# Token mixers: a lane's own next step traced at a higher priority for VectorE, ScalarE and GpSimd

## The chip, the core and the metric

The kernel runs on one core of a Trainium2 chip. The metric is the device time of one execution in microseconds (us). The core's engines are TensorE (PE, matrix products), VectorE (DVE), ScalarE (ACT, functions by table), GpSimd (POOL) and SyncE (SP, which issues the DMAs here). Each takes its own instructions in a fixed order; what must wait for another engine waits on a semaphore, and everything behind it on that engine waits too.

## The reference

A model of two blocks over 512 tokens of width 1024 in float32. The first block mixes tokens in four groups side by side, each 256 wide, and ends with a convolutional gated feed-forward; the second has a short convolution, a gated feed-forward, latent attention and another one. The change lies in the first block's mixers:

```python
def token_mix(h, w_in, ...):
    p = (h @ w_in).astype(jnp.float32)
    (fox_qkv, fox_f, gdn_qkv, gdn_b, gdn_a, gdn_z, hg_q, hg_f, hg_i, hg_g,
     gla_qk, gla_v, gla_gk, gla_g) = jnp.split(p, _cut_points(IN_SIZES), axis=-1)
    ...
    o_a = rms_norm(fox_attention(q, k, split_heads(v, FOX_HEADS), log_f), fox_on_g)
    ...
    o_b = gated_delta_chunked(l2norm(split_heads(q, GDN_HEADS)), l2norm(split_heads(k, GDN_HEADS)),
                              split_heads(v, GDN_HEADS), g, beta)
    ...
    o_c = gla_chunked(jax.nn.silu(split_heads(hg_q, HG_HEADS)), k_in, split_heads(hg_i, HG_HEADS),
                      log_forget, HG_DK ** -0.5)
    ...
    o_d = gla_chunked(split_heads(q, GLA_HEADS), split_heads(k, GLA_HEADS), split_heads(gla_v, GLA_HEADS),
                      split_heads(log_a, GLA_HEADS), GLA_DK ** -0.5)
    ...
    return jnp.concatenate([merge_heads(o_a), merge_heads(o_b), merge_heads(o_c), merge_heads(o_d)], axis=-1)
```

`gated_delta_chunked` solves a triangular system in chunks of 64 tokens, `gla_chunked` needs the products q·k with a decay for each pair of positions.

## The kernel before, in words

Activations lie with features on the partitions, 512 tokens on the free axis. A large product (128 rows of the result) takes eight steps over the 1024 inputs, three matmuls each: the weights `raw` come by DMA, ScalarE rounds them to `wh` (L111) and VectorE takes the rest `wl` (L112), and the matmuls are wh·xh, wh·xl and wl·xh. They gather in a PSUM tile `mm`, which an eviction on VectorE scales into SBUF (L901 for most, L927 a gate, L935 ahead of a convolution, L228).

While the 28 blocks of `w_in` are multiplied, the mixers run beside them in `Mix.conduct` (L751 on). There are three lanes, each a list of generators that follow one another: l (`hg` and `gla`, both through `la`), g (the delta rule, `gdn`) and f (attention, `fox`). The running generator of a lane is a `Strand` in the list `strands`; the ends of the mixers (normalising and gating, `finish`) run as further generators in `self.beside`. Each generator yields the time after which its next step is due by the planner's clock `self.clk`. In every round `conduct` either lets one due generator trace its next step (L804, `t = next(due.gen, None)`) or traces one step of a `w_in` product. Both lie in a `manual_schedule` for TensorE (L1556): TensorE's order is the order of tracing. On VectorE, ScalarE and GpSimd the order is made by the framework's scheduler: among instructions that are ready by its own model it takes the one with the lowest priority number, and that number counts up as the program is traced. So of two that are ready, the one traced earlier goes first.

Each lane has two PSUM tiles in turn (`lps`, `gps`, `fps`; L642 to L644) and temporaries `s`, `u`, `sq` in rings of three or four.

The steps that matter here:

- `la` makes the score products between k and q of a chunk in seven levels. `la_level` (L1287 on) prepares one: GpSimd subtracts the decay (L1299, `s`), ScalarE takes two exponentials of it (L1300, L1301), GpSimd multiplies k by one half (L1303, `lw`), and VectorE multiplies q by the other half, one instruction for each head (L1310, `lbd`, two or four). Then TensorE multiplies `lw` and `lbd` into an `lps` tile, and the result is copied into the scores `lat` under a mask on VectorE (L1361), or on ScalarE at the first level (L1359). The level after the next is prepared behind that copy. Ahead of the levels stand the products lps<-lq,lk with their masking (L1334), the running sums `lg` (L1338), and in `hg` the copy of the values `lv` out of an `lps` tile on ScalarE (L1268).
- `gdn` makes for each of two heads a decay matrix `gmt` (four exponentials on ScalarE, L1088), the weighted products `gat` and `gmt` (L1031), the copy `gmr` (L1107) and the start `gxt` of the inverse (L1110, L1111); GpSimd scales `gko` (L1115) and later masks `gmt` (L1131). Six rounds follow, each with `gy` (L1137), `gx` (L1141) and `gxt` (L1143) out of `gps` tiles. `gvn` (L1117) is the scaled values. At the end `gst` holds the state.
- `la` ends with the states `lst` (L1401).

Of the kernel before, what the change touches and what calls it, by code (L numbers as in the profile page):

```python
# [1 line left out]

# [1 line left out]

# [659 lines left out]
class Mix(Mla):  # L664
# [93 lines left out]
    def conduct(self, jobs, lanes):  # L758
# [7 lines left out]
        strands = [None] * len(lanes)  # L766
# [6 lines left out]
        while True:  # L773
# [6 lines left out]
            due = next((s for s in live if s.at <= self.clk), None)  # L780

            while held and "mean" in self.over:
                ps, name, post = held.pop(0)
                t = post(ps)
# [16 lines left out]
                        due_row = self.clk + DUE  # L801
            if due and not (dense and self.clk - fed > FEED):
                self.lane = due.rings
                t = next(due.gen, None)  # L804
                self.lane = {}
                due.at = self.clk + (t or 0.0)
                if t is None:
                    if due in strands:
                        strands[strands.index(due)] = None
                        self.over.add(due.name)  # L810
                        ready[due.name] = self.clk
                    else:
                        self.beside.remove(due)
                continue
# [873 lines left out]
```

## Time and profile before

| what | before |
|---|---|
| median of three runs | 1862.54 us (1862.07 to 4696.66) |
| the profiled execution | 1862.47 us, span 1860.8 us |
| TensorE busy | 1822.3 us (98% of the span) |
| VectorE busy | 1050.7 us (56%) |
| ScalarE busy | 737.8 us (40%) |
| GpSimd busy | 194.4 us (10%) |
| stage of the mixers beside w_in | about 50 to 376 us |
| in it: TensorE, VectorE, ScalarE, GpSimd busy | 314.67, 242.96, 149.77, 82.97 us |

How to read it: the profiled execution is one of the program's executions, and its span runs from its first to its last instruction. "Busy" is the time in which an engine executes, and the rest is idle time, most of it waiting. TensorE works nearly all the time, so the idle time of another engine costs nothing unless TensorE waits for it. Two matmuls overlap, so starts are a better measure than the listed durations. The granted clock (PEclk) is the share of full speed that the chip gave TensorE. The time 4696.66 is that of one run of the three and lies far off the two others; the profiled execution is near those two.

### The profile page before, as it was taken

To read this page: it belongs to the slowest core of one execution; us is meant where nothing else is said; L and a number is where in the kernel's file an instruction comes from. 1 tells how busy PE (TensorE), PEld (TensorE's weight loads), DVE (VectorE), ACT (ScalarE), POOL (GpSimd) and SP (SyncE) were. 2 spreads that over 40 slices of the span, in tenths; PEclk is the share of its full clock that TensorE was granted. 3 is DMA by queue.
4 is the path that set the end of the run, shared out by engine and by line. 5 is a ranking of instruction groups with operands and counts; after the bars stand their busy time and mean duration, and the time that the engine had idled before them with its cause. 6 is when DMAs were issued, how large, how long until landed. Compare 5 with 4: busy or idle time off the path is not lost.

```text
span 1860.8 us, 22057 instructions
## 1 busy us (share of the span) xinstructions
PE 1822.3 (98%) x8609; PEld 1501.5 (81%) x8609; DVE 1050.7 (56%) x1627; ACT 737.8 (40%) x1138; POOL 194.4 (10%) x225
## 2 busy tenths in 40 slices
PE   8999999999999999999999999999999999999997
PEld 6787887778888888888888888888777888888886
DVE  7875985767777633455564444333876454444323
ACT  6543544544444422322343233322577333232322
POOL 1510502210000001011200000011011200000001
PEclk9999999999999999999999999999999999999999
DMA  4111101332323333323232323333222222323332
GB/s 167 57 35 46 46 35 35 106 101 91 102 93 100 90 100 94 102 91 102 92 106 92 102 91 102 94 94 97 71 60 74 79 96 97 102 91 99 94 94 76
DMA packets 53223, 162.61 MB, mean 87 GB/s; under 512 B 6528, under 2 KB 13184, under 8 KB 53120
## 3 DMA queue, kind: packets, MB, share of 16 engines
q1 hardware_dynamic: 52992, 161.21, 27.2%
q8 instruction: 67, 1.10, 0.3%
q14 instruction: 36, 0.29, 0.0%
q10 hardware_dynamic: 128, 0.01, 0.0%
HBM read 157.78 MB, written 2.10 MB: 86 GB/s over the span
## 4 chain that ended last, share of the span: by engine, by line
PE 85%; DVE 9%; ACT 3%; issue 1%; POOL 1%; DMA 0%; SPq 0%; DVEq 0%; ACTq 0%; POOLq 0%
PE mm L125 24%; PE mm L127 24%; PE mm L126 24%; PE mm L705 6%; PE gps L705 3%; PE lps L705 1%; PE fps L705 1%; DVE lbd L1310 1%; ACT wh L111 1%; DVE wl L112 1%; DVE lat L1361 1%; PE ps L577 1%; DVE ptl L112 0%; PE ps L165 0%; DVE nm L580 0%
## 5 line engine op out<-in xcount | busy, mean ns | idle before, releaser
L111 ACT ACTIVATE wh<-raw 128x1024 fp32r<-128x1024 f32 (+3 forms) x308 | 308.6, 1003 | 762.6 <-PE mm L126 463.5
L125 PE MATMUL mm<-xh,wh 128*128 128x512 f32 x1336 | 521.8, 391 | 0.4 <-ACT xh L173 0.4
L126 PE MATMUL mm<-xl,wh 128*128 128x512 f32 x1336 | 520.7, 390 | 0.5 <-DVE xl L174 0.5
L127 PE MATMUL mm<-xh,wl 128*128 128x512 f32 x1336 | 519.9, 389 | 0.0
L112 DVE TENSOR_TENSOR wl<-raw,wh 128x1024 fp32r<-128x1024 f32 (+3 forms) x300 | 361.0, 1203 | 224.8 <-ACT wh L111 221.6
L126 PEld LDWEIGHTS mm<-xl,wh 128*128 128x128 f32 x1336 | 250.8, 188 | 54.9 <-DVE xl L174 1.4
L125 PEld LDWEIGHTS mm<-xh,wh 128*128 128x128 f32 x1336 | 250.8, 188 | 53.7 <-issue 1.0
L127 PEld LDWEIGHTS mm<-xh,wl 128*128 128x128 f32 x1336 | 250.8, 188 | 51.9 <-issue 0.2
L125 PE MATMUL mm<-hidh,wh 128*128 128x512 f32 (+1 forms) x614 | 236.7, 386 | 0.0
L127 PE MATMUL mm<-hidh,wl 128*128 128x512 f32 (+1 forms) x614 | 235.3, 384 | 0.0
L126 PE MATMUL mm<-hidl,wh 128*128 128x512 f32 (+1 forms) x614 | 233.8, 381 | 0.0
L127 PEld LDWEIGHTS mm<-hidh,wl 128*128 128x128 f32 x614 | 115.4, 188 | 24.2
L126 PEld LDWEIGHTS mm<-hidl,wh 128*128 128x128 f32 x614 | 115.4, 188 | 23.6
L705 PE MATMUL mm<-xh,wh 128*128 128x512 f32 x291 | 127.7, 439 | 6.6 <-ACT xh L173 5.8
L125 PEld LDWEIGHTS mm<-hidh,wh 128*128 128x128 f32 x614 | 115.5, 188 | 21.9 <-ACT wh L111 0.2
L705 PE MATMUL mm<-xh,wl 128*128 128x512 f32 x291 | 116.0, 398 | 1.6 <-DVE wl L112 1.6
L705 PE MATMUL mm<-xl,wh 128*128 128x512 f32 x291 | 116.1, 399 | 0.4 <-DVE xl L112 0.4
L278 DVE TENSOR_TENSOR u<-mm,rb 128x512 f32<-128x512 f32 x44 | 30.4, 691 | 141.2 <-PE mm L127 141.2
L158 POOL TENSOR_TENSOR z<-z,sq 128x512 f32<-128x512 f32 x31 | 50.9, 1643 | 556.6 <-ACT sq L156 518.9
L274 DVE TENSOR_TENSOR u<-mm,rb 128x512 f32<-128x512 f32 x44 | 30.4, 691 | 90.9 <-PE mm L127 90.8
L111 ACT ACTIVATE hidh<-s 128x512 fp32r<-128x512 f32 x66 | 41.8, 633 | 88.6 <-DVE s L255 57.5
L705 PEld LDWEIGHTS mm<-xh,wh 128*128 128x128 f32 x291 | 56.1, 193 | 18.8 <-ACT xh L173 6.3
(434 smaller groups left out, 2089.2 us busy)
## 6 DMA issues: line engine op xcount, KB each, us to landing
raw<-in_w_a_dram SPq DMA_DIRECT2D x52, 512.0 KB, 3.3
raw<-in_w_b_dram SPq DMA_DIRECT2D x52, 512.0 KB, 3.4
raw<-in_w_up_dram SPq DMA_DIRECT2D x44, 512.0 KB, 3.3
raw<-in_w_in_dram SPq DMA_DIRECT2D x28, 512.0 KB, 3.3
raw<-in_conv_w_in_dram SPq DMA_DIRECT2D x24, 512.0 KB, 3.3
raw<-in_w_down_dram SPq DMA_DIRECT2D x16, 448.0 KB, 3.4
raw<-in_w_a_dram SPq DMA_DIRECT2D x16, 448.0 KB, 3.3
raw<-in_w_b_dram SPq DMA_DIRECT2D x16, 448.0 KB, 3.3
```

The lines of the kernel that those rows point to most:

```text
L111: nc.scalar.activation(out=h, in_=src, func=ACTF.Copy)
L112: (eng or nc.vector).tensor_tensor(out=l, in0=src, in1=h.bitcast(F32), op=ALU.subtract)
L125: nc.tensor.matmul(out=ps, lhsT=h, rhs=xh, start=(k == 0), stop=False)
L126: nc.tensor.matmul(out=ps, lhsT=h, rhs=xl, start=False, stop=False)
L127: nc.tensor.matmul(out=ps, lhsT=l, rhs=xh, start=False, stop=(k == kt - 1))
L158: eng.tensor_tensor(out=acc, in0=acc, in1=sq, op=ALU.add)
L274: nc.vector.tensor_tensor(out=g, in0=ps, in1=r, op=ALU.mult)
L278: nc.vector.tensor_tensor(out=g, in0=ps, in1=r, op=ALU.mult)
L577: nc.tensor.matmul(out=ps[:, :n], lhsT=l[:, qs], rhs=r[:, :n], start=(i == 0), stop=False)
L705: self.nc.tensor.matmul(out=out, lhsT=lhsT, rhs=rhs, start=start, stop=stop)
L1310: nc.vector.tensor_tensor(out=bd[rows, :, h].rearrange("p c (n j) -> p c n j", j=b), in0=c4(q)[rows], in1=c4(d)[rows], op=ALU.mult)
L1361: nc.vector.copy_predicated(out=at.rearrange("p c (n j) -> p c n j", j=2 * b)[:, :, :, b:], mask=self.lmask[:, lv - 1].rearrange("p (n j) ...
```

## The change

One statement of `conduct` is changed. While it lets a lane's running generator trace its next step, the scheduler's priority is set back to that of the program's start (`high_priority()` without an offset), and restored behind the step. The numbers count up from there within the step, so that every lane step begins with the same number, whatever its age. The generators of `beside`, the products of w_in with their splits and evictions, and all that follows keep their numbers. TensorE's order, made by hand, is the same, and so is SyncE's. Line numbers behind the change are two higher.

```diff
--- before.py
+++ after.py
@@ -1,4 +1,4 @@
-from contextlib import ExitStack, contextmanager
+from contextlib import ExitStack, contextmanager, nullcontext
 
 import numpy as np
 
@@ -801,7 +801,9 @@
                         due_row = self.clk + DUE
             if due and not (dense and self.clk - fed > FEED):
                 self.lane = due.rings
-                t = next(due.gen, None)
+
+                with self.tc.high_priority() if due in strands else nullcontext():
+                    t = next(due.gen, None)
                 self.lane = {}
                 due.at = self.clk + (t or 0.0)
                 if t is None:
```

What it does to the order is seen at two places. In all rows the first name is what is written, the names behind the arrow are what is read, and the number behind a name tells one buffer from another.

The first place is the start of `hg` for the first pair of heads, with the first levels of `la_level` (`s_685`, `s_692`, `s_786`, `s_823`, `s_865`, in the order of the levels) beside `gdn` (`gko`, `gmt_571`). GpSimd's order there before:

```order
L1299 TENSOR_TENSOR s_685<-lg_643 128x512
L1299 TENSOR_TENSOR s_692<-lg_643 128x512
L1115 TENSOR_TENSOR gko_527<-gko_527,gkof_559 128x512
L1303 TENSOR_TENSOR lw0_228<-lk_507,s_685 128x4x64
L1299 TENSOR_TENSOR s_786<-lg_643 128x512
L1299 TENSOR_TENSOR s_823<-lf_500 128x512
L1375 TENSOR_TENSOR lqi_1057<-lq_465,lqi_1057 128x512
L1303 TENSOR_TENSOR lw1_229<-lk_507,s_692 128x8x32
L1131 TENSOR_TENSOR gmt_571<-gmt_571,strict_191 128x512
L1299 TENSOR_TENSOR s_865<-lf_500 128x512
```

and after the change:

```order
L1301 TENSOR_TENSOR s_685<-lg_643 128x512
L1117 TENSOR_TENSOR gko_527<-gko_527,gkof_559 128x512
L1377 TENSOR_TENSOR lqi_1057<-lq_465,lqi_1057 128x512
L1301 TENSOR_TENSOR s_692<-lg_643 128x512
L1301 TENSOR_TENSOR s_786<-lg_643 128x512
L1301 TENSOR_TENSOR s_823<-lf_500 128x512
L1305 TENSOR_TENSOR lw0_228<-lk_507,s_685 128x4x64
L1305 TENSOR_TENSOR lw1_229<-lk_507,s_692 128x8x32
L1301 TENSOR_TENSOR s_865<-lf_500 128x512
L1133 TENSOR_TENSOR gmt_571<-gmt_571,strict_191 128x512
```

The mask of `gmt_571` stood ahead of `s_865` and now stands behind it, and `lqi` and `gko` have moved up. ScalarE at the same place before:

```order
L1300 ACTIVATE s_786<-s_786 128x16x16
L1301 ACTIVATE s_786<-s_786 128x16x16
L1300 ACTIVATE s_823<-s_823 128x32x8
L1301 ACTIVATE s_823<-s_823 128x32x8
L1268 ACTIVATE lv_597<-lps_637 128x512
L1107 ACTIVATE gmr_631<-gmt_571 128x512
L1088 ACTIVATE gmt_655<-gps_649,gbias_530 128x128 x4
L1300 ACTIVATE s_865<-s_865 128x64x4
```

and after:

```order
L1303 ACTIVATE s_786<-s_786 128x16x16
L1303 ACTIVATE s_823<-s_823 128x32x8
L1303 ACTIVATE s_692<-s_692 128x8x32
L1302 ACTIVATE s_865<-s_865 128x64x4
L1270 ACTIVATE lv_597<-lps_637 128x512
L1303 ACTIVATE s_865<-s_865 128x64x4
L1109 ACTIVATE gmr_631<-gmt_571 128x512
L1090 ACTIVATE gmt_655<-gps_649,gbias_530 128x128 x4
```

The copy `lv_597` out of its `lps` tile stood ahead of the exponentials of `s_865`, and now stands behind the first of them.

The second place is VectorE in `la` with four heads (`gla`), beside the start of `gdn` for the second pair: `lbd0` and `lbd1` are the two buffers of prepared levels, and the numbers behind `lps` tell which product a `lat` copy reads. The row with x4 stands for four instructions. Before:

```order
L1310 TENSOR_TENSOR lbd0_226<-lq_1393,s_2107 32x4x64 x4
L901 TENSOR_TENSOR rq_2122<-mm_2015,rb_291 128x512
L1031 SCALAR_TENSOR_TENSOR gat_2129<-gps_2124,gik_1958,gmt_2095 128x128 x4
L112 TENSOR_TENSOR wl_2137<-raw_2134,wh_2136 128x1024
L1361 COPY_PREDICATED lat_1790<-lmask_203,lps_2144 128x16x8
L1361 COPY_PREDICATED lat_1803<-lmask_203,lps_2144 128x16x8
L1361 COPY_PREDICATED lat_1816<-lmask_203,lps_2144 128x16x8
L1361 COPY_PREDICATED lat_1847<-lmask_203,lps_2144 128x16x8
L1031 SCALAR_TENSOR_TENSOR gmt_2095<-gps_2151,gik_1958,gmt_2095 128x128 x4
L1361 COPY_PREDICATED lat_1790<-lmask_203,lps_2169 128x16x8
L1110 TENSOR_TENSOR u_2163<-gmt_2095,mixb_193 128x512
L1361 COPY_PREDICATED lat_1803<-lmask_203,lps_2169 128x16x8
```

There follow `gxt_2162`, two more copies of `lps_2169`, the four of `lbd1` and then `gvn_1929`. After:

```order
L1363 COPY_PREDICATED lat_1790<-lmask_203,lps_2169 128x16x8
L1363 COPY_PREDICATED lat_1803<-lmask_203,lps_2169 128x16x8
L1363 COPY_PREDICATED lat_1816<-lmask_203,lps_2169 128x16x8
L1363 COPY_PREDICATED lat_1847<-lmask_203,lps_2169 128x16x8
L1119 TENSOR_TENSOR gvn_1929<-gps_2187,gnk_1964 128x512
L1112 TENSOR_TENSOR u_2163<-gmt_2095,mixb_193 128x512
L1312 TENSOR_TENSOR lbd1_227<-lq_1393,s_2176 32x4x64
L1113 TENSOR_TENSOR gxt_2162<-u_2163,mlac_181 128x512
L1312 TENSOR_TENSOR lbd0_226<-lq_1393,s_2107 32x4x64
L1312 TENSOR_TENSOR lbd1_227<-lq_1393,s_2176 32x4x64 x2
L1312 TENSOR_TENSOR lbd0_226<-lq_1393,s_2107 32x4x64 x2
L1312 TENSOR_TENSOR lbd1_227<-lq_1393,s_2176 32x4x64
```

One instruction of `lbd0` (`s_2107`) stands ahead of this piece, before `gat_2129`; the three others stand at its end, among those of `lbd1`, where all four stood in a block ahead of the copies of `lps_2144`.

## Rows read from the trace of the kernel before

**Rows 1.** Windows: stretch; length; busy of PE, PEld, DVE, ACT, POOL; PEclk; DMA.

```profile
50.00:376.00 326.00, 314.67 (x1828) 261.13 (x1827) 242.96 (x539) 149.77 (x308) 82.97 (x82) 0.98 0.16 53
376.00:1400.00 1024.00, 1020.58 (x4535) 838.76 (x4533) 564.55 (x725) 393.27 (x537) 76.64 (x102) 1.00 0.30 93
```

**Rows 2.** Waits of PE, 40 to 376 us: total us, times, longest us.

```profile
PE gps L705 <- DVE gxt L1143: 1.9, 4, 0.6
PE lps L705 <- DVE lat L1361: 1.7, 1, 1.7
...
PE lps L705 <- DVE finr L1004: 0.6, 1, 0.6
...
PE lps L712 <- DVE lf L1278: 0.3, 1, 0.3
```

**Rows 3.** PE's instructions at 68 us: start us, us, count, [idle before <-releaser].

```profile
64.24 0.38 PE L705 MATMUL gps<-mixb,identb 128*128 128x512 bf16 x1 [1.53 <-DVE gat L1031]
...
68.10 1.16 PE L705 MATMUL lps<-lq,lk 64*128 64x128 f32 x8
```

**Rows 4.** ScalarE's instructions, 49 to 75 us.

```profile
55.49 0.87 ACT L1088 ACTIVATE gmt<-gps,gbias 128x128 f32<-128x128 f32 x3
...
66.48 0.58 ACT L1268 ACTIVATE lv<-lps 128x512 f32<-128x512 f32 x1
```

**Rows 5.** GpSimd's instructions, 57 to 76 us.

```profile
58.02 3.05 POOL L1299 TENSOR_TENSOR s<-lg 128x512 f32<-128x512 f32 x2 [5.34 <-DVE gkof L1071]
...
62.03 1.71 POOL L1303 TENSOR_TENSOR lw<-lk,s 128x256 f32<-128x256 f32 x1
...
67.81 0.92 POOL L1303 TENSOR_TENSOR lw<-lk,s 128x256 f32<-128x256 f32 x1
68.69 1.61 POOL L1131 TENSOR_TENSOR gmt<-gmt,strict 128x512 f32<-128x512 f32 x1
70.25 1.22 POOL L1299 TENSOR_TENSOR s<-lf 128x512 f32<-128x512 f32 x1
```

**Rows 6.** VectorE's instructions, 217 to 232 us.

```profile
219.42 2.17 DVE L1310 TENSOR_TENSOR lbd<-lq,s 32x256 f32<-32x256 f32 x4
...
224.40 0.88 DVE L1361 COPY_PREDICATED lat<-lmask,lps 128x128 f32<-128x128 uint8 x4
...
230.52 0.69 DVE L1117 TENSOR_TENSOR gvn<-gps,gnk 128x512 f32<-128x512 f32 x1
```

**Rows 7.** PE's instructions, 223 to 240 us.

```profile
224.01 1.03 PE L705 MATMUL lps<-lbd,lw 128*128 128x256 f32 x4
...
227.84 1.02 PE L705 MATMUL lps<-lbd,lw 128*128 128x256 f32 x4
```

**Rows 8.** PE's instructions with a wait, 238 and 264 us.

```profile
238.42 1.13 PE L705 MATMUL lps<-lbd,lw 128*128 128x256 f32 x4 [1.15 <-DVE gate L1022]
...
264.74 0.63 PE L705 MATMUL gps<-gxt,gy 128*128 128x64 f32 x4 [0.45 <-DVE gxt L1143]
```

**Rows 9.** VectorE's instructions, 258 to 270 us.

```profile
264.60 1.16 DVE L1401 SCALAR_TENSOR_TENSOR lst<-lst,lea,lps 32x64 f32<-32x64 f32 x4
```

**Rows 10.** VectorE's instructions, 104 to 113 us.

```profile
107.67 0.70 DVE L143 SCALAR_TENSOR_TENSOR sq<-sq 128x512 f32<-128x512 f32 x1
```

**Rows 11.** PE's instructions, 106 to 111 us.

```profile
108.75 0.63 PE L705 MATMUL gps<-gy,gxt 128*128 128x64 f32 x4 [0.96 <-DVE gx L1141]
```

**Rows 12.** ScalarE's instructions, 329 to 336 us.

```profile
330.16 1.28 ACT L261 ACT_TABLE_LOAD   x1
```

**Rows 13.** Windows, as in rows 1, about the two stretches of lower clock.

```profile
106.00:110.70 4.70, 3.38 (x19) 2.62 (x19) 4.68 (x9) 0.00 (x0) 0.53 (x1) 1.00 0.00 0
110.70:114.10 3.40, 3.40 (x11) 2.83 (x11) 3.37 (x6) 1.78 (x2) 0.00 (x0) 0.50 0.00 0
...
291.60:298.40 6.80, 6.80 (x23) 5.51 (x24) 4.73 (x8) 5.70 (x8) 4.59 (x4) 0.50 0.25 78
```

**Rows 14.** The page's costliest groups: count, busy us, mean ns, idle before.

```profile
L112 DVE TENSOR_TENSOR wl<-raw,wh 128x1024 fp32r<-128x1024 f32 (+3 forms) x300 | 361.0, 1203 | 224.8 <-ACT wh L111 221.6
```

## The prediction

> **What bounds the kernel now.** I read first the windows by stage: in the stage of the token mixers, 50 to 376 us, TensorE is busy 314.67 of 326 us, and in the 1024 us behind it 1020.58 [rows 1]. The reader is to see that TensorE is the bound everywhere and that the change, which touches only the mixers' lanes, can win back no more than TensorE's idle time in that stage, 326 − 314.67 = 11.3 us, 0.6% of the span. The view of TensorE's waits says who is waited for: thirteen kinds, from gxt (1.9 us in four waits) to lf (0.3 us), add up to 12.5 us (they overlap the modelled ends of matmuls a little) [rows 2]. Nearly all are single waits of 0.2 to 1.7 us for VectorE, each at a known place. So I do not price "lanes first" as a whole: I go to each place where the order of the changed program differs, and ask which instruction TensorE's next product then waits for.
>
> **What the change does to the order.** While a lane's step is traced, its priority is counted from the program's start. The step's first instruction competes as number 0, the next as 1, and so on. So lane work passes weight splits, evictions and finishes, as is meant; but two steps of lanes no longer stand by age: the first instruction of a young step passes the fourth of an old one. TensorE's and SyncE's rows are the same, so products wait in the same sequence as before, and no DMA is issued at another place in its queue.
>
> **Place 1, at 68 us: a loss.** TensorE waits 1.53 us for gat at 64.24 and starts the product lps_673 at 68.10 [rows 3]. gat (VectorE) now stands ahead of a weight split, which removes the 1.53. But lps_673 needs ScalarE's copy lv_597 out of the older lps tile, 0.58 us at 66.48 [rows 4], and ScalarE's order now puts the exponential of s_865 ahead of lv_597; it waits for GpSimd's s_865, the ninth of GpSimd's rows of this stretch. When does that end? GpSimd worked without a pause from 58.02 to the end of s_865 at 70.25 + 1.22 = 71.47; its order now lets gmt_571 (68.69 to 70.25, 1.56 us) go behind s_865: 12.2 + 1.2 − 1.56 = 11.9 us of work [rows 5]. It starts later: three gmt exponentials (0.87 us) [rows 4] now stand ahead of the two small functions that end lf, so 58.02 becomes about 58.9. s_865 then ends at 70.8; 0.3 us for the issue of its exponential, 0.58 for lv_597: lps_673 starts at 71.7, 3.6 us later. The other bound: lf no later (−0.9), and GpSimd's lw at 0.92 us, as at 67.81, rather than 1.71 and its first two subtractions at 2 × 1.22 rather than 3.05 (−1.4 together) [rows 5] gives 69.4, +1.3. I take +3.0, near the rows as they ran, because VectorE's work beside GpSimd is the same in kind. The removed wait at 64.24 is already in this: lps_673's start is set by lv_597, whenever TensorE arrives.
>
> The same lw took 1.71 and 0.92 us here [rows 5]. [...]
>
> **Place 2, at 228 us: a loss.** VectorE's four multiplications lbd0 (s_2107) stood as one block at 219.42, 2.17 us [rows 6], long ahead of their reader, the product lps_2209 at 227.84 [rows 7]. Now one stands there; the other three stand behind lat_2169, gvn, u, gxt and among the four of the next level. lat_2169 can't start before its product ends: 224.01 + 1.03 = 225.04 [rows 7]. From there, at the distances between starts in the rows: four lat copies 0.8, gvn 0.6, u and gxt, of gvn's shape, 0.6 each, first lbd1 0.6 to 0.9, then six more multiplications at 0.42 to 0.54 (2.17 / 4) [rows 6] = 5.7 to 6.7, less the last lbd1 (0.4 to 0.5), which nobody waits for here: 5.3 to 6.2. lps_2209 starts at 230.4 to 231.2 instead of 227.84: +2.5 to +3.4, taken as +2.9. Nothing hides it: what follows on TensorE stands behind it. The weight split wl that is passed there has room: it is moved some 9 us back and its first reader comes some 9 us after its old end, and moves 2.9 us with the rest.
>
> **Place 3, at 238 us: a gain.** lps at 238.42 waited 1.15 us for an eviction (gate) [rows 8] that held its psum tile; by the new order it needs a lat copy instead, which is there. −1.1.
>
> **Place 4, at 265 us: a loss.** The four state updates lst (1.16 us) [rows 9] now pass gxt, for which TensorE already waited at 264.74 [rows 8]. Less the time that TensorE has between, +0.9 (0 to 1.2).
>
> **Place 5, at 108 and 131 us: gains.** gx passes one lat copy and the step of L143 at 107.67 (0.70 us) [rows 10], and TensorE's wait of 0.96 at 108.75 goes [rows 11]. The product behind it still waits for gxt, which comes earlier by L143's time alone, less what overlaps: −0.6. The wait for gxt at 131 us, 0.5 by the mean of gxt's four (1.9 / 4) [rows 2], goes, since gx and gxt pass a convolution: −0.5.
>
> **Place 6, at 335 and 353 us: gains.** The single wait for finr (0.6) goes, since that product needs a copy of ScalarE instead of an eviction; the single wait for lat (1.7) [rows 2] loses the one split of about 0.6 us that it stood behind. −1.2.
>
> Two more table loads on ScalarE (at about 295 and 333 us) stand in the sum with nothing: at both places the next product waits for a GpSimd result that comes later than ScalarE's. If that cover is gone, each costs up to its own time, 1.28 us by the row of one [rows 12].
>
> **Sum.** +3.0 + 2.9 − 1.1 + 0.9 − 0.6 − 0.5 − 1.2 = +3.4. Against the profiled execution's 1862.47 us (span 1860.8 and 1.7 around it; 0.07 under the median): 1865.9. With the lower bounds, +1.3 + 2.5 − 1.1 + 0 − 2.3 = +0.4; with the upper, +3.6 + 3.4 − 1.1 + 1.2 − 2.3 = +4.8.
>
> **The rivals.**
> *The intended gain prevails.* It decides at places 1 and 2: if the exponential of s_865 and the three lbd0 are in time (GpSimd faster still beside an emptier VectorE, VectorE waiting less than the rows say), what is left is −1.1 − 0.6 − 0.5 − 1.2 = −3.4: 1859. Then also the stretch at half clock behind 110.7 may go. For it: the gains are places where the trace names the wait. Against: both losses are chains of strict order, each longer than the time it has. With only one of them averted: 1862 to 1863.
>
> *The clock falls.* [...] One new stretch gives 1867.6 to 1869.3, two 1869.3 to 1872.7, and the one at 110.7 vanishing takes 1.7 off. Against it: at 64.24 a wait of 1.53 us [rows 3] led to no half clock. [...]
>
> *Slower by over 2%: the w_in products starve.* Splits, evictions and convolutions now stand behind any ready lane step. One wl takes 1.2 us of VectorE [rows 14]; if each of 28 blocks of w_in came that late, TensorE would lose 28 × 1.2 = 34 us, to 1896, and with an eviction's time on each over the bound of 37. It decides where VectorE has no slack; it is busy 242.96 of 326 us [rows 1], so it catches up, and the split passed at place 2 has time to spare.
>
> That the change does nothing is excluded: the order of three engines changes.
>
> **How the numbers follow.** The sum as worked out, with or without one place averted (1862 to 1867.5): 0.58. The gain prevails (1856 to 1861.9): 0.2. The clock falls (1867.5 to 1873): 0.2. Starving: 0.02. The likeliest is 1865.8; its own range 1862 to 1867.5. The range that leaves two in ten out takes the nearer half of both neighbours: 1859 to 1871. 2% is 37 us (about what a measurement of this kernel can tell from no change), more than three times TensorE's idle time in the stage, so faster 0.01, slower 0.02, same 0.97.
>
> **What would show it.** In the profile after: ScalarE idle ahead of the exponential of s_865 near 69 us, and TensorE waiting 3 us or more for lv (L1268, two lines lower after) just behind; no wait for gat at 64; a wait of some 3 us for lbd near 228; no wait for gate at 238 and for finr at 335; shorter ones for gx and gxt at 109 and 131; from 376 us on the same durations as before. GpSimd's nine rows much under 10.5 us would prove place 1 wrong, lbd0 complete before 228 place 2. A granted clock below 1 behind 72 or 231 us would be the clock's rival. TensorE waiting for wl or wh often would be the starving.

## The result, and the profile after

The changed kernel takes 1872.05 us (median of four runs, 1871.44 to 1873.12) against 1862.47 us, the median of four runs of the kernel before made with them: a ratio of 1.0054, with a 95% interval of 1.0041 to 1.0067. It is slower by 8 to 12 us, about half a per cent. One of those four runs (4696.66 us) and one of not_l below (3053.95 us) lie far off, and the ratios leave them out. The profiled execution is the slowest of the four, 1873.12 us with a span of 1871.0; against the span of before, 1860.8, that is +10.2.

The windows of the profile after (stretch; length; busy of PE, PEld, DVE, ACT, POOL; granted clock; DMA), to be held against [rows 1]:

```profile
50.00:376.00 326.00, 306.28 (x1775) 253.69 (x1774) 243.83 (x526) 147.41 (x302) 80.59 (x81) 0.97 0.14 49
376.00:1400.00 1024.00, 1021.09 (x4531) 839.15 (x4529) 562.33 (x717) 390.11 (x525) 75.67 (x102) 1.00 0.29 95
```

TensorE is busy 8.4 us less in the same 326 us, and from 376 us on as before. So all of it was lost in the mixers, as forecast. The waits of TensorE there (40 to 390 us; total us, times, longest us), to be held against [rows 2]:

```profile
PE lps L705 <- ACT lv L1270: 4.2, 1, 4.2
PE lps L705 <- DVE lbd L1312: 3.1, 1, 3.1
PE mm L705 <- DVE xl L112: 1.9, 2, 1.3
PE lps L705 <- DVE lat L1363: 1.9, 2, 1.1
PE gps L705 <- DVE gx L1143: 1.8, 2, 1.2
PE gps L705 <- DVE gxt L1145: 1.5, 2, 0.9
PE mm L705 <- DVE z L937: 1.1, 1, 1.1
...
PE gps L712 <- DVE gxt L1113: 1.0, 1, 1.0
PE mm L705 <- DVE wl L112: 0.9, 2, 0.5
...
PE gps L712 <- DVE u L1009: 0.8, 1, 0.8
```

The first two lines are places 1 and 2 of the forecast. The waits for gat, for gate and for finr are gone, and those for the gxt of the rounds (L1143 before) fell from 1.9 to 1.5 us. But z, u and the first gxt (L1113) are not in the list of before, xl was there with 0.4 us, and no term of the forecast has them. The windows about the two long waits and behind them:

```profile
62.70:71.00 8.30, 4.12 (x25) 3.22 (x25) 6.84 (x10) 3.26 (x9) 7.18 (x7) 1.00 0.19 63
71.30:78.10 6.80, 6.80 (x25) 5.54 (x24) 3.84 (x7) 2.13 (x7) 2.60 (x2) 0.50 0.00 0
228.00:235.30 7.30, 4.75 (x25) 3.66 (x24) 7.02 (x20) 1.23 (x2) 2.66 (x2) 0.99 0.00 1
235.30:242.10 6.80, 6.28 (x20) 5.19 (x20) 3.83 (x10) 1.75 (x3) 2.87 (x3) 0.51 0.24 77
...
303.40:306.80 3.40, 3.40 (x12) 2.31 (x11) 2.87 (x4) 3.37 (x5) 2.79 (x3) 0.50 0.00 0
```

Where each of the two waits ends, a stretch of 6.8 us at half clock begins (a granted clock of 0.50; the 128x512 products start 0.43 us apart in it and 0.23 outside); the one at 110.7 [rows 13] is gone, and the one near 292 is half as long. In the mixers that makes 17.1 us at half clock against 10.2.

Since TensorE's order is the same in both programs, the start of each of its products can be taken from both traces and subtracted. What the difference gains or loses from place to place is the account of the 10.2 us:

| place (us in before) | what | forecast | measured |
|---|---|---|---|
| 64 to 68 | wait for gat gone (−1.5), wait for lv (+4.3) | +3.0 | +2.8 |
| 69 to 73 | half clock from 71.3 to 78.1 of after | rival | +3.1 |
| 78 | gxt (L1111 of before) late | not seen | +1.1 |
| 109 and 110 | gx earlier, gxt now waited for | −0.6 | −0.7 |
| 111 to 114 | half clock gone | 0 | −1.4 |
| 130 and 131 | gx and gxt earlier | −0.5 | −1.2 |
| 196 and 197 | z and wl late | not seen | +2.0 |
| 228 | three lbd late | +2.9 | +3.2 |
| 228 to 231 | half clock from 235.1 to 241.9 of after | rival | +2.9 |
| 236 and 238 | gate no longer waited for, lat instead | −1.1 | −0.8 |
| 262 to 265 | lst, and gx behind fk | +0.9 | +1.2 |
| 292 to 298 | half clock shorter | 0 | −1.6 |
| 335 and 353 | finr; lat | −1.2 | −1.3 |
| 337 | u of a finish late | not seen | +0.9 |
| 356 | xl late | not seen | +1.4 |
| elsewhere | | 0 | about −1.4 |

The places that the forecast priced sum to +3.2 (forecast +3.4). The four that it did not see sum to +5.4, and the clock to +3.0.

**Place 1 in the rows.** ScalarE's instructions of after, then GpSimd's, then TensorE's (start us, us, count, [idle before <-releaser]):

```profile
69.91 0.42 ACT L1302 ACTIVATE s<-s 128x256 f32<-128x256 f32 x1 [1.03 <-POOL s L1301]
70.23 0.58 ACT L1270 ACTIVATE lv<-lps 128x512 f32<-128x512 f32 x1
```

```profile
58.79 2.03 POOL L1301 TENSOR_TENSOR s<-lg 128x512 f32<-128x512 f32 x1 [5.92 <-DVE gkof L1073]
...
68.85 1.03 POOL L1301 TENSOR_TENSOR s<-lf 128x512 f32<-128x512 f32 x1
```

```profile
70.86 1.74 PE L705 MATMUL lps<-lq,lk 64*128 64x128 f32 x8 [4.18 <-ACT lv L1270]
```

ScalarE stands idle for s_865, and lv is next behind it. GpSimd began at 58.79 (forecast 58.9) and ended s_865 at 69.88, so its nine rows took 11.1 us where 11.9 was the upper and 10.5 the lower bound. TensorE's product starts at 70.86, 2.8 us later than the 68.10 of [rows 3].

**Place 2 in the rows.** VectorE's instructions of after, and TensorE's:

```profile
229.82 0.89 DVE L1363 COPY_PREDICATED lat<-lmask,lps 128x128 f32<-128x128 uint8 x4 [0.22 <-PE lps L705]
...
232.84 3.17 DVE L1312 TENSOR_TENSOR lbd<-lq,s 32x256 f32<-32x256 f32 x6
```

```profile
235.82 2.05 PE L705 MATMUL lps<-lbd,lw 128*128 128x256 f32 x4 [3.07 <-DVE lbd L1312]
```

From the first lat copy to the release of the product 6.0 us pass (forecast 5.3 to 6.2).

**Two places that the forecast did not see.** At 196 us of before, VectorE in before, then in after, and TensorE behind it:

```profile
189.31 3.42 DVE L1310 TENSOR_TENSOR lbd<-lq,s 32x256 f32<-32x256 f32 x4 [1.12 <-ACT s L1301]
...
193.38 0.68 DVE L935 TENSOR_TENSOR z<-mm,rb 128x512 f32<-128x512 f32 x1
```

```profile
195.70 3.71 DVE L1312 TENSOR_TENSOR lbd<-lq,s 32x256 f32<-32x256 f32 x5
199.45 0.69 DVE L1336 TENSOR_TENSOR lat<-lps,mlac 128x512 f32<-128x512 f32 x1
200.06 0.68 DVE L937 TENSOR_TENSOR z<-mm,rb 128x512 f32<-128x512 f32 x1
200.65 1.21 DVE L112 TENSOR_TENSOR wl<-raw,wh 128x1024 fp32r<-128x1024 f32 x1
```

```profile
200.88 0.47 PE L705 MATMUL mm<-xh,wh 128*128 128x512 f32 x1 [1.12 <-DVE z L937]
```

z is an eviction that frees the PSUM tile of the next w_in product, and the weight split wl stands behind it. In the kernel before, four lbd and one lat stood ahead of z in this stretch. Now it is eight and two: three lbd and a lat from 192.45 on, and the five lbd and the lat above. So the lbd of one more level, and one more lat, have passed it. And at 78 us, VectorE in after, then GpSimd, then both in before:

```profile
80.78 0.69 DVE L1119 TENSOR_TENSOR gvn<-gps,gnk 128x512 f32<-128x512 f32 x1 [0.31 <-PE gps L712]
...
83.12 1.66 DVE L1113 TENSOR_TENSOR gxt<-u,mlac 128x512 fp32r<-128x512 f32 x1
```

```profile
82.22 2.02 POOL L1133 TENSOR_TENSOR gmt<-gmt,strict 128x512 f32<-128x512 f32 x1 [7.90 <-DVE u L1112]
```

```profile
76.80 0.68 DVE L1111 TENSOR_TENSOR gxt<-u,mlac 128x512 fp32r<-128x512 f32 x1
77.40 0.68 DVE L1117 TENSOR_TENSOR gvn<-gps,gnk 128x512 f32<-128x512 f32 x1
```

```profile
75.89 2.62 POOL L1131 TENSOR_TENSOR gmt<-gmt,strict 128x512 f32<-128x512 f32 x1 [2.94 <-ACT sq L1435]
```

Two things differ. First, gvn stood behind gxt and now stands ahead of it. Second, gxt is an instruction of 0.67 us in after too, where GpSimd does nothing beside it (at 227.10). Here it takes 1.66 and ends at 84.78, some 0.5 us behind GpSimd's gmt, which ran beside it. But the same two instructions met in the kernel before as well, and there gxt took 0.68 us and gmt 2.62; at 232.16 of after a pair of the same kind ran side by side, and gxt took 0.67 us, gmt 1.80. Which of the two takes longer isn't told by the kinds alone, and why gxt took 1.66 us here isn't shown. TensorE came free at 83.98 (84.93 less a wait of 0.95), and a gxt of 0.68 us would have ended at 83.80: by the rows it was the long gxt that TensorE waited for in after. In not_hg0 and not_l, described below, gxt took 0.68 us, stood behind gvn too, and TensorE still waited 0.66 and 0.67 us for it. So the order alone can cost something here. No run was made for this pair.

### The profile page after: what moved, and what is told of

The parts are those of the page before. It is cut to its first block, busy times and chain, and to the rows that moved or that the text cites. A ratio compares the mean times of both kernels' runs of the same rounds, so it can differ in the third digit from the quotient of the medians.

```text
span 1871.0 us, 22049 instructions
## 1 busy us (share of the span) xinstructions
PE 1823.9 (97%) x8609; PEld 1501.9 (80%) x8609; DVE 1057.0 (56%) x1627; ACT 740.3 (40%) x1140; POOL 192.5 (10%) x225
## 4 chain that ended last, share of the span: by engine, by line
PE 86%; DVE 8%; ACT 3%; issue 2%; POOL 1%; DMA 0%; SPq 0%; DVEq 0%; POOLq 0%; ACTq 0%
PE mm L125 24%; PE mm L127 24%; PE mm L126 24%; PE mm L705 7%; PE gps L705 3%; PE lps L705 2%; PE fps L705 1%; DVE lbd L1312 1%; DVE wl L112 1%; ACT wh L111 1%; DVE lat L1363 0%; PE ps L577 0%; POOL s L1301 0%; DVE xl L174 0%; DVE ptl L112 0%
```

## The experiments

The kernels of the table below edit the one line of the change, and nothing else; TensorE's order is the same in all of them. A run's time hangs on how much half clock it got: the 31 runs of the kernel before in one comparison have spans of 1857.0 us at a mean granted clock of 0.998 to 1865.4 at 0.992. So beside the time stands the mean of span times granted clock over a kernel's runs, which takes out what the half clock adds, and a little more (the clock is given to 0.001, 1.9 us in one run; a stretch of 6.8 us cost 2.9 to 3.1 us above, and the product takes out 3.4). For before it is 1851.7 to 1852.4 us, for after 1857.4. The kernels were timed in several comparisons, each with runs of before of its own, whose medians go from 1860.81 to 1862.76 us; the ratios are free of that, differences of medians between comparisons are not.

| kernel | raised | median us | ratio to before, 95% | span × clock, mean |
|---|---|---|---|---|
| after | all lanes, to the start | 1872.05 | 1.0041 to 1.0067 | 1857.4 |
| not_hg0 | all but hg0 | 1867.84 | 1.0030 to 1.0063 | 1856.3 |
| not_l | lanes g and f | 1867.71 | 1.0019 to 1.0045 | 1852.6 |
| offset | all lanes, by 1000 | 1874.87 | 1.0051 to 1.0096 | 1857.3 |
| only_l | lane l | 1873.71 | 1.0050 to 1.0100 | 1861.3 |
| only_hg0 | hg0 | 1866.85 | 1.0013 to 1.0041 | 1853.8 |
| only_gla_gdn1 | gla and gdn1 | 1865.82 | 1.0009 to 1.0028 | 1854.7 |
| offset10 | all lanes, by 10 | 1869.63 | 1.0019 to 1.0046 | 1855.4 |
| rounds | gdn from its rounds on | 1864.27 | 0.9995 to 1.0033 | 1849.8 |

### Which lanes, and is it the age?

not_hg0:

```diff
-                with self.tc.high_priority() if due in strands else nullcontext():
+                with self.tc.high_priority() if due in strands and due.name != "hg0" else nullcontext():
```

> The change as made, but the steps of the generator hg0 keep their ordinary priority; by its order ScalarE's copy lv_597 is again ahead of the exponentials of s_865 (place 1, 68 us), while lbd0 of s_2107 still stands in pieces among the next level's (place 2, 228 us). Theory A (the two places where a lane's steps lost their age cost the time, each with the stretch at half clock behind it): the wait of 4.2 us for lv is gone, and with it the half clock from 71.3 to 78.1; net -2.8 for the wait and -3.1 for the clock, 1872 - 6 = 1866 us; the wait of 3 us for lbd and the half clock behind it stay. Rival B (the time goes where products of w_in wait for passed splits and evictions: z 1.1, wl 0.9, xl 1.9, u 0.8, about 5 us in the waits after): 1869 to 1872, those waits as before. Rival C (the wait costs, but the half clock doesn't hang on it): 1869.

Measured: 1867.84 us, 4.2 less than after by the medians. But the intervals of the two ratios overlap for the most part, so by time alone the gain isn't shown. Of the waits of TensorE in the profile:

```profile
PE lps L705 <- DVE lbd L1312: 3.1, 1, 3.1
...
PE lps L705 <- DVE lst L1403: 1.1, 2, 0.8
...
PE lps L705 <- ACT lv L1270: 0.4, 1, 0.4
```

The wait for lv shrank from 4.2 to 0.4 us, and no half clock stands at 71; the wait for lbd is unchanged. Rival C (the half clock does not hang on the wait) would have left it at 71. Theory A's 1866 isn't reached: two waits for lst (1.1 us, 0.3 in after) take the place of some of the gain, and new stretches of 3.4 us at half clock come at 271.2 and 356.5. The wait for lbd, as long as in after, was followed by 3.4 us at half clock here (230.2 to 233.6) instead of 6.8.

not_l:

```diff
+                with self.tc.high_priority() if due in strands and due.rings is not L_LANE else nullcontext():
```

> The change as made for the lanes g and f alone; lane l (hg0, gla, hg1) keeps its ordinary priority. By its order both lv_597 and lbd0 stand as before the change. Theory A: both long waits and both half clocks behind them gone, 1872 - 6 - 6 = 1860 us, 2 below the kernel before, if the gains at 109, 131 and 335 us stay. Rival B: 1864 to 1868, since the lanes g and f still pass the splits and evictions. Rival C: 1866.

Measured: 1867.71 us. Both long waits are gone, but the time is that of not_hg0. The waits, and one window:

```profile
PE lps L705 <- DVE lst L1403: 3.5, 2, 2.7
PE lps L705 <- DVE lat L1363: 2.8, 2, 1.7
```

```profile
263.50:287.40 23.90, 23.90 (x93) 21.50 (x92) 10.85 (x30) 5.14 (x17) 0.62 (x2) 0.51 0.07 23
```

Theory A's number (1860) falls. Rival B's number (1864 to 1868) has the time, but not by rival B's waits: those for the splits wl and xl are 0.5 and 0.4 us, as before the change, and none is for z. The raised lanes g and f pass lane l, whose lst and lat now come late; behind the wait of 2.7 us for lst, TensorE had half clock for 23.9 us although it was busy all the time. By span times clock this kernel is where the kernel before is (1852.6): most of what it loses is clock.

offset:

```diff
+                with self.tc.high_priority(offset=1000) if due in strands else nullcontext():
```

> All lane steps raised, but by a fixed 1000 numbers instead of to the program's start, so that two lane steps still stand by age. By its order lbd0 is whole again and ahead of the next level's (place 2), but lv_597 still stands behind the first exponential of s_865 (place 1). Theory A: place 2's wait and its half clock are gone, place 1's stay: 1872 - 6 = 1866 us. If age between steps were all that the change lost (rival D), it should give back all: 1860 or less. Rival B: 1869 to 1872, since splits and evictions are passed just as much.

Measured: 1874.87 us, as slow as after or slower. Its waits:

```profile
PE mm L705 <- DVE wl L112: 4.4, 3, 2.8
...
PE lps L705 <- ACT lv L1270: 2.2, 1, 2.2
```

With the age of the lane steps kept, the wait for lbd is gone, as expected, and the one for lv is half as long; but the waits for wl grow from 0.9 to 4.4 us: VectorE starts one split at 242.22 only, behind seven lbd and eight lat copies that it ran from 235.19 on. Rival D (the lost age is all) falls, and theory A's 1866 with it. Rival B's mechanism, that products of w_in wait for passed splits, is seen in this kernel, which takes even longer than its 1869 to 1872.

only_l:

```diff
+                with self.tc.high_priority() if due in strands and due.rings is L_LANE else nullcontext():
```

> Only lane l is raised to the program's start; g and f keep their priority. By its order lv_597 stands behind both exponentials of s_865 (place 1 a little worse), lbd0 is whole (place 2 as before the change). Theory A: place 1's wait of 4 us or a little more and a half clock behind it, no wait for lbd near 230: 1866 us, and the gains that come from lane g (gx and gxt at 109 and 131 us) missing: up to 1868. Rival B: near 1863 to 1865, since two lanes of three pass nothing.

Measured: 1873.71 us, almost 6 more than the upper number of theory A. The wait for lbd near 228 us is gone, as expected, and the late z is there:

```profile
PE mm L705 <- DVE z L937: 1.1, 1, 1.1
```

The raised lane passes what the others need: lbd of later levels pass the eviction lv, for which TensorE waits 3.9 us at 61 us, and gat and gmt of lane g, 1.6 and 2.4 us near 216 and 227 us.

### The two places alone, and smaller steps

only_hg0 and only_gla_gdn1:

```diff
+                with self.tc.high_priority() if due in strands and due.name == "hg0" else nullcontext():
...
+                with self.tc.high_priority() if due in strands and due.name in ("gla", "gdn1") else nullcontext():
```

> Place 1 alone: only the generator hg0 is raised to the program's start; by its order lv_597 stands behind both exponentials of s_865, and lbd0 of s_2107 stands whole, as before the change. Theory A': each place where an older lane step is passed costs its own wait, and what the raised steps win elsewhere is small; the half clock comes in stretches of 3.4 us behind waits, more or fewer in each execution. Then: a wait of 3 to 5 us for lv or for what lv waits for near 61 to 71 us, span without half clock 1855.7 (before, likewise) + 3 to 4, and with one to three stretches 1864 to 1868 us. Theory E (raising hg0 is harmless; the changed program lost at place 1 only because GpSimd was also busy for the raised lane g): no wait over 1 us there, 1859 to 1863.

> Place 2 alone: only gla and gdn1 are raised; lv_597 stands as before the change, lbd0 of s_2107 stands in pieces among the next level's. Theory A': no wait for lv; the wait of 3 us for lbd near 228 us, with z and wl late at 196 us (1.5 us, if it was gla's lbd that passed them); span without half clock + 3 to 5 against before, time 1864 to 1869. Theory E: the lbd wait is there only when hg0 and gdn0 are raised too: none over 1 us, 1859 to 1863.

Measured: 1866.85 and 1865.82 us. Raised alone, hg0 makes TensorE wait once more for what its own first copy needs, though for another part of it: VectorE's two lbd (2.73 us) stand ahead of the eviction lv. First VectorE's rows of only_hg0, then TensorE's:

```profile
61.87 2.73 DVE L1312 TENSOR_TENSOR lbd<-lq,s 64x256 f32<-64x256 f32 x2
64.62 0.69 DVE L903 TENSOR_TENSOR lv<-mm,rb 128x512 f32<-128x512 f32 x1
```

```profile
65.37 0.81 PE L712 MATMUL lps<-mlac,lv 128*128 128x128 f32 x4 [3.88 <-DVE lv L903]
```

The waits of only_gla_gdn1:

```profile
PE lps L705 <- DVE lbd L1312: 3.1, 1, 3.1
...
PE mm L705 <- DVE z L937: 1.1, 1, 1.1
```

Here are place 2, whole, and the late z, with neither hg0 nor gdn0 raised. The late z stands in both kernels that raise gla without most of the rest, this one and only_l, so it belongs to gla's steps. Place 2 stands here but not in only_l, which raises gla without gdn1: it takes both. Place 1 went when hg0's steps were left as they were (not_hg0); raised alone they lose at another row, the one above. Theory E falls. The times are those of theory A', but by span times clock the two lose 1.8 and 2.7 us against 1852.0, less than its 3 to 4 and 3 to 5.

offset10:

```diff
+                with self.tc.high_priority(offset=10) if due in strands else nullcontext():
```

> All lane steps raised by 10 numbers only, about one step of a product. By its order lv_597 stands as before the change and lbd0 is whole, a few rows moved; some 120 rows of VectorE still differ. Theory F (TensorE reads in the order of tracing, so the ordinary priority is by the time at which a result is needed, and what is passed comes too late in proportion to how far it is passed): near the kernel before, within 3 us of it, span without half clock 1854 to 1857. Rival (any raising of lanes over splits and evictions loses, however far): +5 us or more, like the offset of 1000.

Measured: 1869.63 us, and span times clock 1855.4, 3.4 more than before. By the time, theory F's number (within 3 us of before) falls, and that of its rival holds (5 us or more, however far the lanes are raised); by span times clock, theory F's 1854 to 1857 holds. This run doesn't decide between them. A raise of ten numbers already costs about two thirds of what the change costs.

rounds:

```diff
+                with self.tc.high_priority() if due in strands and due.name + ".kv" in self.over else nullcontext():
```

> Only the six rounds of the delta rule (gy, gx, gxt), where the trace of before names waits for gx, gxt and gy, are raised to the program's start; everything else keeps its priority. If the gains measured at 109, 131, 239 and 335 us can be had by themselves: 0.7 + 1.2 + about 1 = 2 to 3 us less than before, without half clock 1853; 1857 to 1861 us. By theory F a few waits for lat, lst or splits take their place instead, and the sum is within 2 us of before.

The condition of the edit is true from the rounds on to the end of gdn, so the steps behind the rounds are raised as well. Measured: 1864.27 us, no difference that can be told (0.9995 to 1.0033). Its waits:

```profile
PE lps L705 <- DVE gate L1024: 2.1, 1, 2.1
...
PE lps L705 <- ACT lv L1270: 1.5, 1, 1.5
PE lps L705 <- DVE lst L1403: 1.3, 1, 1.3
```

The waits for gx and gxt at 109 and 131 us are gone, and span times clock is 2 us under before, as expected. But the wait for gate grew from 1.2 to 2.1 us, and waits for lv and lst are new, so that all waits of the profile from 40 to 390 us sum to 13.0 us against 12.5: the gain that the trace of before promised isn't to be seen in them. And its runs had more half clock (0.993 against 0.996 on average). The sum is within 2 us of before, as theory F has it.

### Is the half clock the answer to the waits?

Three kernels put products by a zero matrix into TensorE's order, added to a `mm` product that is under way, so that TensorE is busy while it waits (one VectorE instruction at the start makes the matrix):

```diff
+    def fill(self):
+        for _ in range(FILL.get(self.npe, 0) if self.open else 0):
+            ps, x = self.open
+            self.nc.tensor.matmul(out=ps, lhsT=self.zero, rhs=x, start=False, stop=False)
+        self.npe += 1
...
     def mm(self, out, lhsT, rhs, start=True, stop=True):
+        self.fill()
```

In the first set, `FILL` counted rows of the trace, and since one float32 product can have two rows there (the four lps<-lq,lk at 70.86 have eight), the filling came 9 us behind the wait at 70.86 and 7 to 67 us off elsewhere.

> The kernel after, with products by a zero matrix in TensorE's order at the two long waits alone: 18 of 128x512 (0.23 us each by their distance in the trace) ahead of the product that waits for lv at 70.86, 13 ahead of the one that waits for lbd at 235.82. They add zero to a product that is under way. Every real product waits as before. Theory G (the half clock at 71.3 to 78.1 and 235.2 to 242 is the answer to the two waits): those two stretches are gone, worth half of 13.7 us = 6.8 less a stretch or two elsewhere: 1865 to 1868 us; span times granted clock as in the kernel after, 1857 to 1858, since the waiting itself stays. Rival H (the stretches have another cause, and come anyway): 1871 to 1873.

> The kernel before, with 4 such products ahead of the wait at 108.75 and 2 each ahead of those at 290.36 and 291.60; nothing else differs in the order of any engine. Theory G: no half clock at 110.7 and 291.6; 1857 to 1859 us, in each run, against 1859 to 1865 for the kernel before, whose runs then differ by the stretches that they got. Rival H: the same as before, 1860 to 1863, with the same spread.

> Only the rounds of the delta rule raised, with 6, 8, 2, 2 and 7 such products ahead of the waits at 68.34, 236.46, 292.15, 293.39 and 352.73. Span times granted clock was 1849.7 us on average for the raised rounds and 1852 for the kernel before, so 2 us less waiting stood against more half clock. Theory G: with the waits filled 1854 to 1858 us, less than the kernel before and than the kernel before with its waits filled. Rival H: 1862 to 1865 as without the filling.

Measured: 1880.75, 1865.64 and 1865.97 us, ratios to before of 1.0090 to 1.0119, 1.0005 to 1.0023 and 1.0008 to 1.0025. These expectations can't be judged, as the products weren't where they say. What they show is the price of filling at a place where TensorE doesn't wait: after_filled's 31 products took 31 × 0.23 = 7 us and it lost 8.7 against after, and its stretches at half clock stayed where they were (70.3 to 77.2, 237.6 to 244.4).

In the second set the filling stands right ahead of the waiting products.

> The kernel after, with 17 products by a zero matrix (0.23 us each by their distance) right ahead of the product that waits for lv, and 12 right ahead of the one that waits for lbd near 236; the waits are 4.18 and 3.07 us, so the products should lie within them. Theory G (the half clock at 71 to 78 and at 235 to 242 is the answer to these waits): neither stretch is there, and the time is 1872 - 6 = 1865 to 1867 us with at most one or two stretches elsewhere; span times granted clock 1857 to 1859, as in the kernel after (1857.4 on average). Rival H (the half clock comes whatever TensorE does in the wait): 1871 to 1873, stretches as before.

Measured: 1868.74 us (1.0021 to 1.0043), 3.3 less than after by the medians; the intervals of the two ratios only just touch. The time lies between theory G's number (1865 to 1867) and rival H's (1871 to 1873); what decides is the profile. The same windows as of after, and TensorE's rows at the first wait:

```profile
62.70:71.00 8.30, 8.09 (x42) 6.35 (x40) 6.84 (x11) 4.71 (x14) 8.30 (x8) 1.00 0.19 63
71.30:78.10 6.80, 6.80 (x42) 5.62 (x42) 5.37 (x15) 3.11 (x7) 1.99 (x2) 1.00 0.00 0
...
235.30:242.10 6.80, 6.62 (x40) 5.50 (x38) 6.51 (x20) 4.65 (x5) 2.29 (x3) 1.00 0.23 80
```

```profile
67.10 4.02 PE L712 MATMUL mm<-xh,zero 128*128 128x512 f32 x17
71.05 1.16 PE L717 MATMUL lps<-lq,lk 64*128 64x128 f32 x8
```

The real product starts at 71.05 where it started at 70.86, so the wait is the same; but the clock is 1.00 behind both, and the product takes 1.16 us instead of 1.74. Theory G is shown for these two stretches: they come with the idle time and go with it, and they cost 3 to 6 us of the change's 10. Span times clock stays high (1859.0), since the waiting stays.

> The kernel before, with 4 such products right ahead of the product that waits 0.96 us for gx at 108.75; nothing else differs in the order of the engines. Theory G: no half clock at 110.7 to 114.1, in the profile and in most runs: 1.7 us less than before at most, 1858 to 1861. Rival H: no difference, 1860 to 1863.

Measured: 1862.64 us (0.9984 to 1.0004). The profile has no half clock from 110.7 to 114.1 (granted clock 1.00 there), as theory G says, and the mean span is 1.5 us under before's 1860.9; in the profiled execution 6.8 us at half clock stand at 237.2, behind a wait of 1.16 us that had none behind it in before (1.15 at 238.42), and 3.4 us at 295.2. In time it can't be told from before, and the number is rival H's (1860 to 1863).

> Only the rounds of the delta rule raised, 6 such products ahead of lps_673 (wait of 1.46 us at 68.34) and 8 ahead of lps_2302 (2.07 us at 236.46). Theory G: no half clock at 69.8 and at 237.1 to 243.9 (10.2 us together, 5.1 of time): 1857 to 1860 us, below the kernel before by 2 to 4; span times granted clock 1850. Rival H: 1863 to 1865 as without them.

Measured: 1862.29 us (0.9992 to 1.0019). No half clock at 69.8 and 237, but one of 6.8 us at 288.4 that no filling covered. Its span times clock is 1851.0, 1.3 us under before, and the time is before's, above theory G's 1857 to 1860. None of the kernels tried beats the kernel before by more than can be measured.

## Why the prediction was wrong

The time, 1872.05 us, lies 6 us above the likeliest and 1 us above the range.

**What held.** The bound and the stage: TensorE, in the mixers alone, with nothing lost behind 376 us. Both losses that the order shows, each with its mechanism and its size: place 1, +2.8 for +3.0; place 2, +3.2 for +2.9. The gains: places 3, 5 and 6 together −4.0 where −3.4 was forecast, most of the difference at 131 us. At 265 us the size was right (+1.2 for +0.9) but the product waited for gx, held up by two fk, rather than for gxt. The two table loads cost nothing. The rival of no effect was rightly excluded. The clock's rival (1867.5 to 1873) has the time, in part by luck: with the clock's +3.0 the forecast's 1865.9 comes to 1868.9 only, and the rest is the places of the next paragraph. One reading was loose, though nothing in the sum hangs on it: not nearly all of TensorE's waits are for VectorE, since ScalarE's gko, wh and sq make 2.6 of the 12.5 us.

**The first step that failed: the list of places was not complete.** The rival of the starving products was set aside with a sentence on the average: VectorE is busy 242.96 of 326 us, "so it catches up". At 196, 337 and 356 us it has no slack within the microsecond or two in which TensorE needs z, wl, u and xl: the last five lbd and a lat take 4.4 us ahead of z. These and the late gxt at 78 us cost 5.4 us, more than the whole forecast sum. only_gla_gdn1 and only_l together show that gla's steps make z late; offset shows how far it can go for the splits (4.4 us for wl). The price of 1.2 us for a split was right, its number of times was not: neither none nor 28.

**The second: the clock was made a rival where it was a term.** The forecast had two new waits of about 3 us, and at two places of before less idle time had been followed by half clock (1.3 of the 4.70 us ahead of 110.7 [rows 13]; waits of 0.53 and 0.60 us ahead of 291.6); yet it gave 0.2 to that, for one counterexample of 1.53 us [rows 3]. Measured, +6.0 behind the two waits and −3.0 from shorter or absent ones elsewhere. The rival's numbers take half its length for a stretch, 1.7 and 3.4 us; no run shows just that: 6.8 us at half clock cost 2.9 to 3.1, and 3.4 us less of it gave 1.4 and 1.6. after_warm shows that the idle time brings the two stretches, so the two places of before were weighed too low. But a wait had no fixed price: the same wait of 3.07 us for lbd was followed by 6.8 us at half clock in after and by 3.4 in not_hg0 and in only_gla_gdn1.

**The third, in part: what GpSimd and VectorE take beside each other was priced at place 1 alone, and from GpSimd's side.** There GpSimd's measured sum, 11.1 us, lay between the bounds. At 78 us, where the forecast has no place, gvn passed gxt, and gxt stood beside GpSimd's mask of the second head and took 1.66 us instead of 0.68; by the rows that cost TensorE 1.1 us. In before the same pair had taken 0.68 and 2.62 us, where after has 1.66 and 2.02. No run tested the pair by itself, so that one of the two makes the other longer isn't shown.

**And the reason behind it was too narrow.** "Two lane steps no longer stand by age" explains lbd at 228 us, but not the loss as a whole: with the age kept (offset) it is as large. A reading that fits, and that no run tests by itself, is that TensorE takes its products in the order of tracing, so that the ordinary priority is already near the order in which results are needed. Every subset that was raised moved something else behind its time: hg0 its own lv, gla z, gla and gdn1 lbd, lanes g and f the lst of lane l, the rounds the gate. That the ordinary order is the best one isn't shown; that none of the nine priorities in the table is measurably better is.

**What stays open.** Why waits of one length are followed by 6.8, 3.4 or 0 us at half clock, why a stretch at half clock lasts 3.4 us in one place and 23.9 in another while TensorE is busy, and why runs of one program differ in how many stretches they get. Why u and xl come late at 337 and 356 us was not followed up.

## What to carry to other kernels

Where one engine's order is fixed and that engine is nearly always busy, the priority by tracing order may be close to a priority by need. Here, raising a class of work over it traded the waits that the trace named for others that it did not show yet. So a forecast needs every instruction that is passed, with the slack at its own reader, and not the named waits and an average load. And a new idle time of TensorE of some microseconds is priced with the half clock that may follow it: in the profile after, that doubled what the two waits cost (+6.0 us for the waits, +6.0 for the clock).

## What was not expected of the hardware

- Seventeen products by a zero matrix held the clock at 1.00 over and behind a wait of 4 us (after_warm) behind which it otherwise fell to 0.50 (after).
- Half clock lasted 23.9 us behind one wait of 2.7 us (not_l), with TensorE busy for 23.90 of them.
- The runs of one unchanged program spread over 8 us (spans of 1857.0 to 1865.4), and their mean granted clock, 0.998 to 0.992, goes with it.
- VectorE's gxt took 1.66 us beside GpSimd's gmt (2.02) in after, and 0.68 beside the same gmt (2.62) in before.
- A wait of 3.07 us for the same lbd was followed by 6.8 us at half clock in one kernel and by 3.4 in two others.
